# Priorities in a planned schedule, and units for two token tiles: a two-layer hybrid decoder on one core

## The chip, the cores and the metric

The kernel runs on one core of a Trainium2 chip. A core has TensorE (PE: matrix products into PSUM), VectorE (DVE), ScalarE (ACT), GpSimd (POOL), and SyncE (SP), whose queue issues nearly all the transfers here. PEld in a profile is TensorE loading the stationary operand of a matmul. The metric is the device time of one execution in microseconds; less is better.

## The reference, cut to what matters

Two layers work on 256 tokens of width 1024, in float32. Each layer does the following:

```
h = rmsnorm(x) * norm_mix
aq, ak, av, iq, ik, iw, hq, hf, hi, hg, ga, gb = split(h @ w_in)
# attention: 8 heads of 64; rope and rmsnorm on aq and ak
score = sum over 4 index heads of iw * relu(iq . ik), causal
keep the 64 best keys of each query, softmax over them, times av -> y_attn
# gated linear recurrence (hgrn): 4 heads of 128, in chunks
f = sigmoid(hf) with a lower bound, k = 1 - f, q = silu(hq), v = hi
S_t = f_t * S_(t-1) + k_t v_t ;  o_t = S_t q_t
y_hgrn = rmsnorm(o) * silu(hg)
x = x + (sigmoid(ga) * (y_attn @ w_pa) + sigmoid(gb) * (y_hgrn @ w_ph)) @ w_out
h = rmsnorm(x) * norm_ffn
x = x + (silu(h @ w_gate) * (h @ w_up)) @ w_ffn_out          # inner width 2816
```

## The kernel before

The 256 tokens are two token tiles of 128 (i = 0, 1; NT = 2 in the code). Every large matrix product is made in three passes to keep float32 accuracy: each operand is split into a part hi and a remainder lo, and hi x hi, lo x hi and hi x lo are added up in PSUM. For the activations the split is made once a layer (hT, yT, mT, h2T, act, each as hi and lo). For the weights it is made on the fly: `take()` (line 523) brings the next chunk of weights, 512 rows of 512 columns in most groups, from memory into a buffer w, ScalarE copies it rounded into hi, and VectorE subtracts to get lo. There are three buffers each for w, hi and lo. `mm3` (line 543) issues the three passes of one 128-row step.

`group` (line 755) makes one of the projections out of two chunks: idx, aq, ak, hf, hq, av, vh, hg, then ga and gb twice, in this order of the weights. For both token tiles the products of one group pile up in two accumulators, PSUM banks of tag P; there are four P banks and four Q banks. An evacuation function then takes the accumulators away with ScalarE: idx to rope and then to the index scores `dot`, aq and ak to norm and rope (`raw`, `rot`, the transposes `qkp`), hf and hq through transposes (`hfp`, `hqp`) to the recurrence, ga and gb to the gates.

The index scores of a token tile go into two Q banks; VectorE forms `work` from them and picks the 64 best by eight rounds of maximum and replace. Then come the logits (`lg`), the softmax in `lm`, its transposes `ptp` into `PT`, and the attention outputs `py`, which are split into yT. The recurrence starts with `hd` and goes through levels (`hl`, `hc`, `hx`) in which TensorE and VectorE alternate, to `po`. Both halves of yT feed `pj`, its result is transposed (`mp`) for `wo`. `out_gemm` (line 1103) does wo and, at the end of a layer, fo; as its last steps, half by half, it adds to x and calls `norm_half` (line 620: multiply by the norm's weight, four transposes xT, split into hi and lo, squares). The FFN runs over 11 blocks of 256 columns: fi, silu times up in `sl`, two transposes `fp` for each token tile, the split into `act`.

Nothing of the order is written by hand. The program is recorded first: each operation, or each `with prog.one()` block on TensorE, is one unit. `path_tails` (line 282) gives each unit the length of the longest way from it to the end, with the costs of a price table; what is not a main matmul counts 1.5 times (`stretch`). `run` (line 297) then simulates the engines: whichever unit can start first is taken, and of those that can start at the same moment on an engine the one with the largest tail plus `rank`, an added number in nanoseconds. A unit starts only when all the buffers that it takes for the first time are free. The orders that come out are fixed in the program; on the chip each engine goes through its own in that order. Small temporaries have the tag s2 (six buffers), larger ones s4 (fourteen).

Before the first data is there TensorE works on `gate`, matmuls of zeros, 28 of them (WARM, line 30). They have the lowest priority of all, so the planner puts one wherever TensorE has nothing else, and they hold one Q bank until the last is done.

The splits of the weights have rank 0 before:

```
        prog.rank = 0.0
        S.activation(hi, w, AF.Copy)
        V.tensor_tensor(lo, w, hi.bitcast(F32), op=ALU.subtract)
```

Of the kernel before, what the change touches and what calls it, by code (L numbers as in the profile page):

```python
# [13 lines left out]
AF = mybir.ActivationFunctionType  # L14
ALU = mybir.AluOpType
# [4 lines left out]
NT = T // 128  # L20
# [6 lines left out]
N_IDX = 324  # L27
C_HQ, C_HF, C_HV, C_HG, C_GA, C_GB = 1860, 2372, 2884, 3396, 3908, 4932
FIRST = {(0, C_IDX): 2, (0, C_AQ): 2}
WARM = 28  # L30
LEVELS = (2, 4, 8)
TWO_PI = 2.0 * np.pi

# [444 lines left out]
def hybrid_trunk(prog, x_d, pos_d, w_in, w_pa, w_ph, w_out, n_mix, n_ffn,  # L478
# [16 lines left out]
    def bank(name, tag="Q"):  # L495
        return prog.tile(tag, [512], F32, name)
# [21 lines left out]
                                     for o in (0, DFF)]) + ([4, 512],))  # L518
        add_rows(w_fo, l, 2, 1024, 0)

    state = {"used": 0}

    def take():
        c = state["used"]
        state["used"] += 1
        a, b, kn = chunks[c]
        k, n = kn or b
        wt, ht, lt = "w" if k * n > 1024 else "s4", "hi", "lo"
        w = prog.tile(wt, [k, n], F32, f"w{c}")
        hi = prog.tile(ht, [k, n], F32R, f"hi{c}")  # L530
        lo = prog.tile(lt, [k, n], F32R, f"lo{c}")
        prog.rank = 5e5 - 1e3 * c
        if kn is None:
            SP.dma_start(w, a)
        else:
            SP.dma_start(w[:, :, 0:256], a)
            SP.dma_start(w[:, :, 256:512], b)
        prog.rank = 0.0
        S.activation(hi, w, AF.Copy)
        V.tensor_tensor(lo, w, hi.bitcast(F32), op=ALU.subtract)  # L540
        return hi, lo

    def mm3(acc, h, hk, wc, wk, wsl, start, stop):
# [57 lines left out]
    def split_to(hi_ap, lo_ap, src, scale=None):  # L601

        if scale is None:
            S.activation(hi_ap, src, AF.Copy)
            V.tensor_tensor(lo_ap, src, hi_ap.bitcast(F32), op=ALU.subtract)
        else:
            S.activation(hi_ap, src, AF.Copy, scale=scale)
            V.scalar_tensor_tensor(lo_ap, src, scale, hi_ap.bitcast(F32), op0=ALU.mult, op1=ALU.subtract)
# [144 lines left out]
    def layer(l, hT, R):  # L753
        last = l == DEPTH - 1
        def group(n, name, evac, kk=4):
            accs = [bank(f"{name}{i}_{l}", "P") for i in range(NT)]
            for c in range(8 // kk):
                wc = take()
                for i in range(NT):
                    for k in range(kk):  # L760
                        kt = c * kk + k
                        mm3(accs[i][:, :n], hT[i], kt, wc, k, slice(0, n), kt == 0, kt == 7)
            for i in range(NT):
                evac(i, accs[i][:, :n])
# [17 lines left out]

        group(N_IDX, "idx", ev_idx, FIRST.get((l, C_IDX), 4))
        bias = []
        for i in range(NT):
            W = (i + 1) * 128
            pds = [bank(f"dot{i}{p}") for p in range(2)]
            with prog.one():
                for j in range(2):
                    for p in range(2):  # L790
                        sl = slice(64 * p, 64 * p + 64)
                        PE.matmul(pds[p][:, j * W:(j + 1) * W], idxT[sl, j, i * 128:(i + 1) * 128], idxT[sl, 2, 0:W],
                                  start=True, stop=True)
            rels = []
            for p in range(2):
                rel = tmp(f"rel{i}{p}", [2, W])
                S.activation(rel, pds[p][:, 0:2 * W].rearrange("p (a b) -> p a b", a=2), AF.Relu)
                rels.append(rel)
            work = prog.tile("work", [256], F32, f"work{i}")[:, :W]
            V.scalar_tensor_tensor(work, rels[0][:, 0, :], idxw[i][:, 0:1], neg[:, 256 - W:256], op0=ALU.mult, op1=ALU.add)  # L800
            for h in range(1, 4):
                V.scalar_tensor_tensor(work, rels[h % 2][:, h // 2, :], idxw[i][:, h:h + 1], work, op0=ALU.mult, op1=ALU.add)
            for r in range(TOPK // 8):
                m8 = small(f"m8{i}")
                V.max(m8[:, 0:8], work)
                V.match_replace(out=work, in_to_replace=m8[:, 0:8], in_values=work, imm_value=REPL)
            b = prog.tile("bias", [256], F32, f"bias{i}")[:, :W]
            V.scalar_tensor_tensor(b, work, REPL, vis[:, 256 - W:256], op0=ALU.is_equal, op1=ALU.mult)
            V.tensor_scalar(b, b, -1.0, BIG, op0=ALU.add, op1=ALU.mult)
            bias.append(b)  # L810
# [28 lines left out]
        group(512, "aq", ev_qk(0, qT), FIRST.get((l, C_AQ), 4))  # L839
        load_g(f"f{l}", n_ffn[l])  # L840
        group(512, "ak", ev_qk(1, kT))


        PT = []
# [73 lines left out]
        def ev_to(dst):  # L918
            def ev(i, acc):
                S.activation(dst[:, i, :], acc, AF.Copy, scale=R[i][:, 0:1])  # L920
            return ev

        group(512, "av", ev_to(av))
        for i in range(NT):
            py = bank(f"py{i}")
            for hp0 in (0, 2):
                with prog.one():
                    for hp in range(hp0, hp0 + 2):
                        for j in range(i + 1):
                            for p in range(2):  # L930
                                h = 2 * hp + p
                                PE.matmul(py[64 * p:64 * p + 64, hp * 128:(hp + 1) * 128], av[:, j, h * 64:(h + 1) * 64],
                                          PT[i][j][:, h, :], start=j == 0, stop=j == i)
            split_to(yT[i][0][:, 0:4, :], yT[i][1][:, 0:4, :], py.rearrange("p (k t) -> p k t", k=4))


        A = big("A", [NT, 4, 128])
# [131 lines left out]
            split_to(yT[i][0][:, 4:8, :], yT[i][1][:, 4:8, :], pv, gc)  # L1069


        gates = {}

        def ev_gate(key):
# [28 lines left out]
        def out_gemm(n_chunks, lhs, gkey, hT_out, name):  # L1103

            accs = [[bank(f"{name}{i}{g}", "Q") for g in range(2)] for i in range(NT)]
            for c in range(n_chunks - 2):
                wc = take()
                for i in range(NT):
                    for k in range(2):
                        (hh, hl), hk = lhs(i, 2 * c + k)  # L1110
                        with prog.one(main=True):
                            for g in range(2):
                                gs = slice(g * 512, (g + 1) * 512)
                                PE.matmul(accs[i][g], hh[:, hk, :], wc[0][:, k, gs], start=c == 0 and k == 0, stop=False)
                                PE.matmul(accs[i][g], hh[:, hk, :], wc[1][:, k, gs], start=False, stop=False)
                            for g in range(2):
                                gs = slice(g * 512, (g + 1) * 512)
                                PE.matmul(accs[i][g], hl[:, hk, :], wc[0][:, k, gs], start=False, stop=False)
            wcs = [take(), take()]
            Rn = []  # L1120
            for i in range(NT):
                ssq = small(f"{name}ss{i}")
                for g in range(2):
                    for c in range(2):
                        for k in range(2):
                            kt = 2 * (n_chunks - 2 + c) + k
                            h, hk = lhs(i, kt)
                            mm3(accs[i][g], h, hk, wcs[c], k, slice(g * 512, (g + 1) * 512), kt == 0, c == 1 and k == 1)
                    xs = x[:, i, g * 512:(g + 1) * 512]
                    V.tensor_tensor(xs, xs, accs[i][g], op=ALU.add)  # L1130
                    if hT_out is not None:
                        norm_half(i, g, gkey, hT_out, ssq, "P")
                    else:
                        SP.dma_start(out_d[0, i * 128:(i + 1) * 128, g * 512:(g + 1) * 512], xs)
                if hT_out is not None:
                    Rn.append(norm_scale(ssq, f"{name}r{i}"))
            return Rn
# [8 lines left out]
        for j in range(11):  # L1146
            accs = [bank(f"fi{i}", "P") for i in range(NT)]
            at = big(f"act{j}", [NT, 2, 2, 128], F32R)
            for c in range(2):
                wc = take()  # L1150
                for i in range(NT):
                    for k in range(4):
                        mm3(accs[i], h2T[i], c * 4 + k, wc, k, slice(0, 512), c == 0 and k == 0, c == 1 and k == 3)
            for i in range(NT):
                pt = bank(f"fp{j}{i}", "Q")
                sl_ = tmp(f"sl{i}", [256])
                S.activation(sl_, accs[i][:, 0:256], AF.Silu, scale=R2[i][:, 0:1])
                V.scalar_tensor_tensor(sl_, accs[i][:, 256:512], R2[i][:, 0:1], sl_, op0=ALU.mult, op1=ALU.mult)
                transpose4(pt, sl_, 2)
                split_to(at[:, i, 0], at[:, i, 1], pt[:, 0:256].rearrange("p (k t) -> p k t", k=2))  # L1160
            acts.append(at)

        hT_n = None if last else pair(f"hT{l + 1}")
# [48 lines left out]
```

## Time and profile before

| | |
|---|---|
| median of 3 runs | 814.75 us (814.44 to 815.56) |
| the profiled execution | 815.19 us, its span 813.4 us |
| TensorE busy | 801.3 us (99%) |
| weight loads (PEld) busy | 657.3 us (81%) |
| VectorE busy | 537.6 us (66%) |
| ScalarE busy | 400.9 us (49%) |
| GpSimd busy | 6.5 us (1%) |
| moved by DMA | 139.66 MB, 172 GB/s in the mean |

The span runs from the first to the last instruction. Busy times are shares of it. All operations are recorded by one helper, so all have line 467 and are told apart by the names of their tiles. A matmul row's duration reaches into the next one, since they are pipelined; the distance from start to start is what it takes from the engine. Layer 0 reaches from 0 to about 410 us, layer 1 from there to the end.

### The profile page before, as it was taken

To read this page: it belongs to the slowest core of one execution; us is meant where nothing else is said; L and a number is where in the kernel's file an instruction comes from. 1 tells how busy PE (TensorE), PEld (TensorE's weight loads), DVE (VectorE), ACT (ScalarE), POOL (GpSimd) and SP (SyncE) were. 2 spreads that over 40 slices of the span, in tenths; PEclk is the share of its full clock that TensorE was granted. 3 is DMA by queue.
4 is the path that set the end of the run, shared out by engine and by line. 5 is a ranking of instruction groups with operands and counts; after the bars stand their busy time and mean duration, and the time that the engine had idled before them with its cause. 6 is when DMAs were issued, how large, how long until landed. Compare 5 with 4: busy or idle time off the path is not lost.

```text
span 813.4 us, 10251 instructions
## 1 busy us (share of the span) xinstructions
PE 801.3 (99%) x3986; PEld 657.3 (81%) x3986; DVE 537.6 (66%) x936; ACT 400.9 (49%) x506; POOL 6.5 (1%) x8
## 2 busy tenths in 40 slices
PE   8989999999999999999999999999999999999998
PEld 7767788888888888888887778888888888888886
DVE  6999856577775455554489997566868645556442
ACT  5764855344364435453356667533445544445330
POOL 3000000000000000000000000000000000000000
PEclk9998999999999999999999999999999999999999
DMA  9725555333656656536546356443354665655531
GB/s 319 248 69 176 186 188 174 104 124 129 219 176 206 195 169 203 170 144 222 168 154 219 111 201 207 155 156 105 108 202 156 206 204 168 199 177 186 169 142 52
DMA packets 86793, 139.66 MB, mean 172 GB/s; under 512 B 3269, under 2 KB 51033, under 8 KB 86745
## 3 DMA queue, kind: packets, MB, share of 16 engines
q1 hardware_dynamic: 86584, 138.94, 51.4%
q8 instruction: 31, 0.51, 0.2%
q14 instruction: 18, 0.14, 0.0%
q10 hardware_dynamic: 160, 0.07, 0.0%
HBM read 137.95 MB, written 1.05 MB: 171 GB/s over the span
## 4 chain that ended last, share of the span: by engine, by line
PE 84%; DVE 10%; issue 2%; ACT 2%; DMA 0%; POOL 0%; POOLq 0%; ACTq 0%; DVEq 0%
PE fi L467 29%; PE fo L467 15%; PE pj L467 5%; PE gb L467 5%; PE wo L467 5%; PE ga L467 4%; DVE lo L467 4%; PE av L467 3%; PE hg L467 3%; PE vh L467 3%; PE hq L467 2%; DVE work L467 2%; PE aq L467 1%; ACT hi L467 1%; PE fp L467 1%
## 5 line engine op out<-in xcount | busy, mean ns | idle before, releaser
L467 DVE TENSOR_TENSOR lo<-w,hi 128x2048 fp32r<-128x2048 f32 (+3 forms) x134 | 296.4, 2212 | 218.5 <-ACT hi L467 217.9
L467 ACT ACTIVATE hi<-w 128x2048 fp32r<-128x2048 f32 (+3 forms) x134 | 247.3, 1846 | 280.7 <-PE fi L467 95.1
L467 PE MATMUL fi<-hi,h2T_hi 128*128 128x512 f32 x352 | 140.8, 400 | 0.2
L467 PE MATMUL fi<-hi,h2T_lo 128*128 128x512 f32 x352 | 137.8, 391 | 0.0
L467 PE MATMUL fi<-lo,h2T_hi 128*128 128x512 f32 x352 | 137.1, 390 | 0.0
L467 PE MATMUL fo<-hi,act 128*128 128x512 f32 x352 | 109.9, 391 | 0.0
L467 PEld LDWEIGHTS fi<-hi,h2T_lo 128*128 128x128 f32 x352 | 66.1, 188 | 15.0 <-DVE h2T_lo L467 0.7
L467 PEld LDWEIGHTS fo<-hi,act 128*128 128x128 f32 x352 | 66.1, 188 | 13.7
L467 PEld LDWEIGHTS fi<-hi,h2T_hi 128*128 128x128 f32 x352 | 66.1, 188 | 13.3 <-DVE h2T_lo L467 0.8
L467 PEld LDWEIGHTS fi<-lo,h2T_hi 128*128 128x128 f32 x352 | 66.2, 188 | 12.6
L467 PE MATMUL fo<-lo,act 128*128 128x512 f32 x176 | 68.5, 389 | 0.0
L467 PEld LDWEIGHTS fo<-lo,act 128*128 128x128 f32 x176 | 33.1, 188 | 6.6
L467 PE MATMUL gb<-hi,hT_hi 128*128 128x512 f32 x64 | 26.7, 418 | 0.0
L467 PE MATMUL wo<-hi,mT_hi 128*128 128x512 f32 x64 | 25.9, 405 | 0.0
L467 PE MATMUL pj<-hi,yT_hi 128*128 128x512 f32 x64 | 25.8, 404 | 0.0
L467 PE MATMUL ga<-hi,hT_hi 128*128 128x512 f32 x64 | 25.7, 401 | 0.0
L467 PE MATMUL wo<-lo,mT_hi 128*128 128x512 f32 x64 | 25.1, 392 | 0.0
L467 PE MATMUL gb<-hi,hT_lo 128*128 128x512 f32 x64 | 25.1, 392 | 0.0
L467 PE MATMUL gb<-lo,hT_hi 128*128 128x512 f32 x64 | 25.0, 391 | 0.0
L467 PE MATMUL ga<-hi,hT_lo 128*128 128x512 f32 x64 | 25.0, 391 | 0.0
L467 PE MATMUL pj<-hi,yT_lo 128*128 128x512 f32 x64 | 25.0, 391 | 0.0
L467 PE MATMUL pj<-lo,yT_hi 128*128 128x512 f32 x64 | 25.0, 390 | 0.0
(340 smaller groups left out, 1302.0 us busy)
## 6 DMA issues: line engine op xcount, KB each, us to landing
w<-in_w_ffn_in_dram SPq DMA_DIRECT2D x88, 512.0 KB, 4.5
w<-in_w_in_dram SPq DMA_DIRECT2D x42, 1024.0 KB, 4.9
w<-in_w_ffn_out_dram SPq DMA_DIRECT2D x22, 1024.0 KB, 4.7
w<-in_w_out_dram SPq DMA_DIRECT2D x8, 1024.0 KB, 4.7
w<-in_w_proj_attn_dram SPq DMA_DIRECT2D x4, 1024.0 KB, 4.9
w<-in_w_proj_hgrn_dram SPq DMA_DIRECT2D x4, 1024.0 KB, 4.8
w<-in_w_in_dram SPq DMA_DIRECT2D x4, 512.0 KB, 4.6
w<-in_w_in_dram SPq DMA_DIRECT2D x4, 324.0 KB, 5.5
```

Source lines behind the costliest of these rows:

```text
L467: getattr(engines[o.eng], name)(*[real(x) for x in a], **{n: real(x) for n, x in k.items()})
```

## The change

The splits of the weights of the groups hf, hq, av, vh and hg get a rank of 2e4, in both layers: `state["ahead"]` is set behind the group ak and set back ahead of the gates. The x add and the norm work in the last steps of `out_gemm` get the same rank. The index scores of both token tiles become one unit on TensorE, which takes four Q banks; the relu, `work` and top-k code behind it is unchanged. The attention outputs of both token tiles become one unit (before: two units for each tile), their splits follow it. In the FFN silu and product of both tiles come first, then all four transposes as one unit into one bank, then one split into hi and lo for both. The matmuls on zeros go from 28 to 24.

```
-WARM = 28
+WARM = 24
+AHEAD = 2e4
...
-    state = {"used": 0}
+    state = {"used": 0, "ahead": 0.0}
...
-        prog.rank = 0.0
+        prog.rank = state["ahead"]
         S.activation(hi, w, AF.Copy)
         V.tensor_tensor(lo, w, hi.bitcast(F32), op=ALU.subtract)
+        prog.rank = 0.0
...
-        for i in range(NT):
-            W = (i + 1) * 128
-            pds = [bank(f"dot{i}{p}") for p in range(2)]
-            with prog.one():
+        dots = [[bank(f"dot{i}{p}") for p in range(2)] for i in range(NT)]
+        with prog.one():
+            for i in range(NT):
+                W = (i + 1) * 128
                 for j in range(2):
                     for p in range(2):
...
-                        PE.matmul(pds[p][:, j * W:(j + 1) * W], idxT[sl, j, i * 128:(i + 1) * 128], idxT[sl, 2, 0:W],
+                        PE.matmul(dots[i][p][:, j * W:(j + 1) * W], idxT[sl, j, i * 128:(i + 1) * 128], idxT[sl, 2, 0:W],
...
         group(512, "ak", ev_qk(1, kT))
+        state["ahead"] = AHEAD
...
+        pys = [bank(f"py{i}") for i in range(NT)]
+        with prog.one():
+            for i in range(NT):
+                for hp in range(4):
+                    for j in range(i + 1):
+                        for p in range(2):
+                            h = 2 * hp + p
+                            PE.matmul(pys[i][64 * p:64 * p + 64, hp * 128:(hp + 1) * 128], av[:, j, h * 64:(h + 1) * 64],
+                                      PT[i][j][:, h, :], start=j == 0, stop=j == i)
         for i in range(NT):
-            py = bank(f"py{i}")
-            for hp0 in (0, 2):
-                with prog.one():
-                    for hp in range(hp0, hp0 + 2):
...
+        state["ahead"] = 0.0
         gates = {}
...
+                    prog.rank = AHEAD
                     xs = x[:, i, g * 512:(g + 1) * 512]
                     V.tensor_tensor(xs, xs, accs[i][g], op=ALU.add)
                     if hT_out is not None:
                         norm_half(i, g, gkey, hT_out, ssq, "P")
                     else:
                         SP.dma_start(out_d[0, i * 128:(i + 1) * 128, g * 512:(g + 1) * 512], xs)
+                    prog.rank = 0.0
...
+            sls = [tmp(f"sl{i}", [256]) for i in range(NT)]
             for i in range(NT):
-                pt = bank(f"fp{j}{i}", "Q")
-                sl_ = tmp(f"sl{i}", [256])
-                S.activation(sl_, accs[i][:, 0:256], AF.Silu, scale=R2[i][:, 0:1])
-                V.scalar_tensor_tensor(sl_, accs[i][:, 256:512], R2[i][:, 0:1], sl_, op0=ALU.mult, op1=ALU.mult)
-                transpose4(pt, sl_, 2)
-                split_to(at[:, i, 0], at[:, i, 1], pt[:, 0:256].rearrange("p (k t) -> p k t", k=2))
+                S.activation(sls[i], accs[i][:, 0:256], AF.Silu, scale=R2[i][:, 0:1])
+                V.scalar_tensor_tensor(sls[i], accs[i][:, 256:512], R2[i][:, 0:1], sls[i], op0=ALU.mult, op1=ALU.mult)
+            pt = bank(f"fp{j}", "Q")
+            with prog.one():
+                for i in range(NT):
+                    for k in range(2):
+                        PE.transpose(pt[:, (2 * i + k) * 128:(2 * i + k + 1) * 128], sls[i][:, k * 128:(k + 1) * 128], ident)
+            split_to(at[:, :, 0], at[:, :, 1], pt.rearrange("p (i k t) -> p i k t", i=2, k=2))
             acts.append(at)
```

## Rows read from the trace of the kernel before

**Rows 1.** The page, part 1: busy us (share of the span) and instructions.

```profile
PE 801.3 (99%) x3986; PEld 657.3 (81%) x3986; DVE 537.6 (66%) x936; ACT 400.9 (49%) x506; POOL 6.5 (1%) x8
```

**Rows 2.** The chain of waits: start us, us, what, with counts.

```profile
201.29 0.87 PE mp L467 x8
...
228.49 1.21 DVE h2T_lo L467 x2
...
353.77 54.43 PE fo L467 x240
```

**Rows 3.** TensorE's timeline in layer 0: start us, us, engine, operation, [idle before <-releaser].

```profile
55.41 0.60 PE L467 MATMUL hfp<-ident,hfraw 128*128 128x128 f32 x4
58.16 0.66 PE L467 MATMUL hfp<-ident,hfraw 128*128 128x128 f32 x4 [2.14 <-ACT hfraw L467]
...
60.32 0.79 PE L467 MATMUL hq<-lo,hT_hi 128*128 128x512 f32 x1 [1.28 <-DVE lo L467]
...
61.34 0.63 PE L467 MATMUL hq<-hi,hT_hi 128*128 128x512 f32 x1
...
66.46 0.44 PE L467 MATMUL hq<-hi,hT_hi 128*128 128x512 f32 x1
```

**Rows 4.** Busy times by stages: us, PE PEld DVE ACT POOL, PEclk, DMA share, GB/s.

```profile
40.00:60.00 20.00, 16.73 (x81) 13.05 (x79) 20.00 (x73) 13.60 (x16) 0.00 (x0) 0.99 0.25 83
60.00:80.00 20.00, 19.68 (x87) 15.70 (x88) 19.00 (x65) 8.55 (x11) 0.00 (x0) 0.84 0.50 160
100.00:120.00 20.00, 20.00 (x101) 16.30 (x100) 12.04 (x16) 10.66 (x13) 0.00 (x0) 1.00 0.50 160
```

**Rows 5.** ScalarE's timeline in layer 0.

```profile
43.25 1.92 ACT L467 ACTIVATE hi<-w 128x2048 fp32r<-128x2048 f32 x1 [0.76 <-PE ak L467]
...
53.51 0.69 ACT L467 ACTIVATE hfraw<-hf,r0y 128x512 f32<-128x512 f32 x1 [0.30 <-DVE rot L467]
```

**Rows 6.** VectorE's timeline in layer 0.

```profile
57.98 2.29 DVE L467 TENSOR_TENSOR lo<-w,hi 128x2048 fp32r<-128x2048 f32 x1
...
101.20 1.23 DVE L467 TENSOR_TENSOR lm<-lm,rs 128x1024 f32<-128x1024 f32 x1
```

**Rows 7.** TensorE's timeline in layer 1, after an hfp unit.

```profile
465.12 0.48 PE L467 MATMUL hq<-hi,hT_hi 128*128 128x512 f32 x1
465.87 0.50 PE L467 MATMUL hq<-lo,hT_hi 128*128 128x512 f32 x1 [0.26 <-DVE lo L467]
```

**Rows 8.** TensorE's timeline around the index scores of token tile 0, layer 1.

```profile
431.36 0.39 PE L467 MATMUL aq<-hi,hT_lo 128*128 128x512 f32 x1
431.68 0.71 PE L467 MATMUL dot<-idxT 64*128 64x128 f32 x8
432.32 0.50 PE L467 MATMUL aq<-hi,hT_hi 128*128 128x512 f32 x1
432.66 0.39 PE L467 MATMUL aq<-lo,hT_hi 128*128 128x512 f32 x1
```

**Rows 9.** TensorE's timeline in the first FFN block of layer 0.

```profile
229.15 0.50 PE L467 MATMUL fi<-hi,h2T_lo 128*128 128x512 f32 x1
229.74 0.50 PE L467 MATMUL fi<-hi,h2T_hi 128*128 128x512 f32 x1
```

**Rows 10.** TensorE's timeline at warm matmuls and at FFN transposes.

```profile
25.85 0.39 PE L467 MATMUL gate<-zero 128*128 128x256 bf16 x2
26.00 0.48 PE L467 MATMUL ak<-hi,hT_hi 128*128 128x512 f32 x1
...
49.00 0.28 PE L467 MATMUL gate<-zero 128*128 128x256 bf16 x1
...
271.80 0.38 PE L467 MATMUL fp<-ident,sl 128*128 128x128 f32 x2
...
274.80 0.38 PE L467 MATMUL fp<-ident,sl 128*128 128x128 f32 x2
```

**Rows 11.** TensorE's timeline at the softmax transposes of tile 1, layer 0.

```profile
122.41 1.04 PE L467 MATMUL ptp<-ident,lm 128*128 128x128 f32 x8
```

More of the change, by code (lines that the diff above doesn't have):

```diff
@@ L791, in layer @@
                         sl = slice(64 * p, 64 * p + 64)
-                        PE.matmul(pds[p][:, j * W:(j + 1) * W], idxT[sl, j, i * 128:(i + 1) * 128], idxT[sl, 2, 0:W],
+                        PE.matmul(dots[i][p][:, j * W:(j + 1) * W], idxT[sl, j, i * 128:(i + 1) * 128], idxT[sl, 2, 0:W],
                                   start=True, stop=True)
+        for i in range(NT):
+            W, pds = (i + 1) * 128, dots[i]
             rels = []
@@ L923, in layer @@
         group(512, "av", ev_to(av))
-        for i in range(NT):
-            py = bank(f"py{i}")
-            for hp0 in (0, 2):
-                with prog.one():
-                    for hp in range(hp0, hp0 + 2):
[L929 to L934, printed above, removed]
+        pys = [bank(f"py{i}") for i in range(NT)]
[7 more added lines that the diff above has]
+                                      PT[i][j][:, h, :], start=j == 0, stop=j == i)
+        for i in range(NT):
+            split_to(yT[i][0][:, 0:4, :], yT[i][1][:, 0:4, :], pys[i].rearrange("p (k t) -> p k t", k=4))
         A = big("A", [NT, 4, 128])
@@ L1153, in layer @@
                         mm3(accs[i], h2T[i], c * 4 + k, wc, k, slice(0, 512), c == 0 and k == 0, c == 1 and k == 3)
+            sls = [tmp(f"sl{i}", [256]) for i in range(NT)]
             for i in range(NT):
-                pt = bank(f"fp{j}{i}", "Q")
-                sl_ = tmp(f"sl{i}", [256])
-                S.activation(sl_, accs[i][:, 0:256], AF.Silu, scale=R2[i][:, 0:1])
-                V.scalar_tensor_tensor(sl_, accs[i][:, 256:512], R2[i][:, 0:1], sl_, op0=ALU.mult, op1=ALU.mult)
-                transpose4(pt, sl_, 2)
-                split_to(at[:, i, 0], at[:, i, 1], pt[:, 0:256].rearrange("p (k t) -> p k t", k=2))
+                S.activation(sls[i], accs[i][:, 0:256], AF.Silu, scale=R2[i][:, 0:1])
+                V.scalar_tensor_tensor(sls[i], accs[i][:, 256:512], R2[i][:, 0:1], sls[i], op0=ALU.mult, op1=ALU.mult)
+            pt = bank(f"fp{j}", "Q")
+            with prog.one():
+                for i in range(NT):
+                    for k in range(2):
+                        PE.transpose(pt[:, (2 * i + k) * 128:(2 * i + k + 1) * 128], sls[i][:, k * 128:(k + 1) * 128], ident)
+            split_to(at[:, :, 0], at[:, :, 1], pt.rearrange("p (i k t) -> p i k t", i=2, k=2))
             acts.append(at)
```

## Prediction

> **What bounds the kernel now.** I read the page first, then the busy table by stages, then the chain of waits, and last TensorE's timeline where the table shows a hole. The page's line gives TensorE 801.3 us busy of 813.4 [rows 1]. That looks like a full engine, but a busy time holds slow matmuls and overlapping records too, so I read start to start instead. In a stretch where nothing else is in the way, 240 matmuls of 128x512 take 54.43 us [rows 2], that is 0.2268 us each; this is TensorE's own rate at the 2.4 GHz level. Transposes stand at 0.87 us for 8, 0.109 us each [rows 2]. What lies above these two prices is lost, and only lost time can be won back, since the change takes away no matrix product that the result needs.
>
> The largest loss is in layer 0 between 55.41 and 66.46 us [rows 3]. In these 11.05 us TensorE issues 8 transposes (hfp) and 15 matmuls of group hq, which at the prices above is 0.87 + 3.40 = 4.27 us. So 6.78 us are lost, in three steps that the reader can see: the second hfp unit waits 2.14 us idle for ScalarE's hfraw, the second hq matmul waits 1.28 us idle for VectorE's lo, and after that the granted clock is at the lower level of 1.2 GHz: 12 matmuls from 61.34 to 66.46 us take 0.427 us each instead of 0.2268. The stage from 60 to 80 us has a mean granted clock of 0.84, the one before it 0.99 [rows 4].
>
> Who is late? ScalarE finished the hi part of the third chunk counted from hf (hf0, hf1, hq0) at 43.25 + 1.92 = 45.17 us [rows 5]. VectorE began its lo part only at 57.98 us [rows 6]: 12.8 us in which it did top-k, rope and newton work, since it was busy for 20.00 of 20 us [rows 4]. So it is the order on VectorE, and not a missing operand, that starves TensorE. (The chunks are counted by the hi parts: with three hi buffers, the hi part that starts at 43.25 us, when hf begins, is the third chunk in the queue.)
>
> Layer 1 has the same place with a small loss: twice, after each hfp unit, the step between two neighbouring hq matmuls is too long and ends with VectorE's lo; one is shown, 0.75 us [rows 7], the other is a little shorter.
>
> **The change part by part.** The profiled execution took 815.19 us, 1.79 us more than its span, and lies 0.44 us above the median of the runs shown. The sum is made against 815.19 and the 0.44 us is taken off at the end.
>
> (1) Priority of 2e4 (20 us in the planner's unit) for hi and lo of the chunks of hf, hq, av, vh and hg. It adds and removes no instruction. A lo of 2048 elements takes 2.2 us; with priority it starts when its hi is there, for hq0 at about 45.2 instead of 57.98 us, for hq1 some 6 us later. The work overtaken is bounded by the three hi buffers: at most three lo, 6.6 us, run ahead of top-k and rope. hq can then follow hf at once and the 6.78 us go, the slow clock with them, because TensorE no longer pauses. I take 6.5, since the two hfp units still have to be visited somewhere. Bounds: 0 (the hole moves) to 6.8. In layer 1 the gap shown is 0.75 us, less the 0.34 us that the first step after a unit of small matmuls takes without any wait [rows 8]: 0.4 us, and for both places 0.8 us, bounds 0 to 1.0.
>
> (2) The norm work and the x add ahead, at the ends of both out projections. At the entry of layer 0's FFN one step between neighbouring fi matmuls is 0.59 us [rows 9], 0.36 too long, right when VectorE does two h2T_lo in 1.21 us after a weight lo [rows 2]. With the norm's work first, the weight lo comes later; fi of the other token tile covers it (12 matmuls, 2.7 us, against 2.2 us of one lo). Two FFN entries of 0.36 make 0.7 us gained. If that cover fails, one lo stands on the path each time: 2.2 us lost. The norm into layer 1 is the same edit; I cost it at nothing, hidden by the idx and aq matmuls, with the same 2.2 us if not.
>
> (3) Both token tiles in one unit. A visit from the main matmuls to a unit of 64-row pieces costs time besides the pieces: the step into dot is 0.32 us and the step after its return 0.34 us [rows 8], against 0.2268, so 0.2 us a visit. dot goes from two visits to one in each layer: 0.4 us. py is not in my rows; its pieces are half-array pieces as well, and by dot's rows the one visit saved in each layer is another 0.4 us. FFN transposes: from one fp visit to the next are 3.00 us [rows 10] for 12 matmuls (2.72) and 2 transposes (0.22): 0.06 us a visit. The 44 transposes of a layer stand in 18 visits (14 of two as in rows 10, 4 of four that hold both tiles already), 11 will be left: 7 x 2 x 0.06 = 0.8 us. Together 1.6 us; bounds 0 (the waits for the second tile eat it) to 2.0. On ScalarE and VectorE two splits of 256 become one of 512, which is off the path in the FFN.
>
> What these units wait for: dot of tile 0 now waits for tile 1's idxT, and behind it wait ScalarE's relu and VectorE's top-k of tile 0; VectorE, with work in its queue for every one of the 20 us from 40 on [rows 4], uses that time for rope. dot now needs all four Q banks at once; the gate bank no longer holds one, because 24 warm matmuls are over in the first microseconds, where 28 had one left at 49.00 us [rows 10]. py of tile 0 waits for the softmax of tile 1.
>
> (4) Four warm matmuls fewer: two of them delay ak by 0.15 us (25.85 to 26.00), one stands between hf matmuls [rows 10]. The ak matmul behind the two waits for a lo anyway, so I take 0.1; bounds 0 to 0.3.
>
> (5) Against all this a term for new lateness. Top-k, rope and newton of layer 0 end up to 6.6 us later while TensorE is 6.5 us earlier. The spare time: VectorE's last softmax product starts at 101.20 us and lasts 1.23 [rows 6], and the transposes that read it are only issued at 122.41 us [rows 11], 20 us later, with VectorE at 12.04 of 20 us in that stage [rows 4]. 20 less 13 leaves 7 us. I take 0.8 us lost for places where the new order fits less well, between 0 and 6 (three lo short of the cover).
>
> Sum: 6.5 + 0.8 + 0.7 + 1.6 + 0.1 - 0.8 = 8.9 us. 815.19 - 8.9 - 0.44 = 805.9, say 806 us. With each term at its better bound it is near 803, with the hole half left near 809.
>
> **The Trainium skill against this.** The first wait of the hole ends with hfraw, and hfraw itself had stood 0.30 us until a VectorE instruction on rot was over [rows 5]; rot is not its operand, so that was a buffer. The Trainium skill, Perfetto Trace Analysis, Identifying Performance Opportunities, says that a gap repeating on the engine that should be saturated can mean that there is no SBUF or PSUM room for the next tile. By that rule priorities would not close the gap; the trace bears it out for 0.30 us and contradicts it for the wait on lo, which has an operand as its releaser. By the rule alone the sum would be that of the first rival.
>
> **Rivals.** *The hole moves* (chance 0.12, 809 to 813 us). The six small temporaries (s2) are held by rope's raw, rot and ropet. If rope ends up to 6.6 us later, hfraw gets its buffer at about 60 instead of 53.5 us, and the accumulators of hf are freed later. hq needs 48 x 0.2268 = 10.9 us, so av asks for these two P banks at about 66.3 us. The margin is 6 us for the first tile and less for the second, which waits in ScalarE's order too. If it is missed by 2 to 4 us, TensorE idles so long, and the clock may fall again (12 matmuls at 0.2 us extra, 2.4 us): 3 to 6 us of the 8.9 are given back.
>
> *No change* (0.05, about 814 to 816): the overtaken work has the higher rank by more than 20 us, lo stays late. Against it: lo was overtaken for 12.8 us only, and even at the stretch of 1.5 that is 19.
>
> *Slower* (0.08, above 817): the attention part comes too late. py of both tiles frees the big buffers from which A and the hgrn chain live; while it waits, only ga and gb feed TensorE. It decides from 7 us of further delay on VectorE beyond the 13 counted; each microsecond after that is one of idle TensorE, and slower in total needs 16 and more, since 8.9 were won first. For it speaks that dot and py of tile 0 both start later than now; against it the 7 us.
>
> **How the numbers follow.** The forecast has 0.75, its own range is 803 to 809. The range that should hold 8 in 10 is 803 to 811: it leaves out the bad half of the first rival, no change and slower (about 0.18 together). A difference of 0.2%, 1.6 us, is about what a measurement of this kernel can tell from no change. Faster: 0.75 + 0.12 = 0.87; within 0.2%: 0.05; slower: 0.08.
>
> **What would show it.** Right: hq follows hf in layer 0 at one matmul each 0.23 us and the granted clock of 60 to 80 us is near 1.00; lo of hq0 starts within 3 us of its hi; fp appears as units of four, 11 in a layer; no gate after the first 9 us. Wrong: a wait on hfraw or on an accumulator between 60 and 75 us; TensorE idle between 125 and 175 us with hd, hl or hc released by VectorE; a wait of the first FFN matmuls on a weight lo; dot released by a late idxT with top-k of both tiles behind it.

## The result, and the profile after

The changed kernel takes 803.3 us (median of 4 runs, 803.1 to 805.65) against 814.88 us before (4 runs, 814.44 to 815.56): a ratio of 0.9864, 95% interval 0.9844 to 0.9883. That is 11.6 us less; the prediction said 806 us and 8.9 us less. The profiled execution took 803.1 us, its span is 801.3.

The first part of the page of the changed kernel: busy us, share of the span, instructions.

```profile
PE 793.1 (99%) x3982; PEld 655.6 (82%) x3982; DVE 535.4 (67%) x914; ACT 399.3 (50%) x486; POOL 5.9 (1%) x8
```

Held against [rows 1], TensorE is at 99% in both. The 12 us don't show as a share; they show from start to start. The timeline of TensorE in layer 0, the place of [rows 3]:

```profile
54.09 0.39 PE L468 MATMUL hf<-hi,hT_lo 128*128 128x512 f32 x1
54.32 0.39 PE L468 MATMUL hq<-hi,hT_hi 128*128 128x512 f32 x1
54.55 0.39 PE L468 MATMUL hq<-lo,hT_hi 128*128 128x512 f32 x1
...
65.58 0.39 PE L468 MATMUL hq<-hi,hT_lo 128*128 128x512 f32 x1
65.80 0.39 PE L468 MATMUL av<-hi,hT_hi 128*128 128x512 f32 x1
```

hq follows hf at 0.23 us, no row carries a wait, and hq as a whole, 48 matmuls and one visit to qkp, takes 54.32 to 65.80: 11.48 us, 0.239 each, the visit counted in. hfp is not between them any more; its eight transposes stand in one visit at 85.7 us. The stages, for [rows 4] (busy us of PE, PEld, DVE, ACT, POOL, granted clock, DMA share, GB/s):

```profile
40.00:60.00 20.00, 20.00 (x93) 16.38 (x92) 20.00 (x51) 9.98 (x11) 0.00 (x0) 1.00 0.58 190
60.00:80.00 20.00, 20.00 (x104) 16.23 (x103) 20.00 (x76) 10.01 (x9) 0.00 (x0) 1.00 0.58 181
```

The same two engines behind it, for [rows 5] and [rows 6]. ScalarE:

```profile
43.41 1.90 ACT L468 ACTIVATE hi<-w 128x2048 fp32r<-128x2048 f32 x1
...
57.59 0.68 ACT L468 ACTIVATE hfraw<-hf,r0y 128x512 f32<-128x512 f32 x1
...
63.22 0.69 ACT L468 ACTIVATE hfraw<-hf,r1y 128x512 f32<-128x512 f32 x1 [0.74 <-DVE ropet L468]
```

VectorE:

```profile
45.84 2.29 DVE L468 TENSOR_TENSOR lo<-w,hi 128x2048 fp32r<-128x2048 f32 x1
51.73 2.28 DVE L468 TENSOR_TENSOR lo<-w,hi 128x2048 fp32r<-128x2048 f32 x1
...
97.50 1.23 DVE L468 TENSOR_TENSOR lm<-lm,rs 128x1024 f32<-128x1024 f32 x1
```

The hi part of hq's first chunk ends at 43.41 + 1.90 = 45.31, its lo begins 0.5 us later; before it was 12.8 us. VectorE is as full as before (20.00 of 20 us in the stage from 40 us on): it does the same work in another order. hfraw is later than before (57.59 against 53.51 us), and the second one has waited for ropet, which is the buffer wait of the prediction's first rival. TensorE does not feel it. And the work that was overtaken is not late here: the last softmax product starts at 97.50 us, before at 101.20 (with the rank of the splits alone it is late, see e1).

TensorE at the new units, for [rows 8] and [rows 10]: index scores and FFN transposes in layer 0, and the attention outputs.

```profile
29.72 1.58 PE L468 MATMUL dot<-idxT 64*128 64x128 f32 x16
31.23 0.50 PE L468 MATMUL aq<-hi,hT_hi 128*128 128x512 f32 x1
...
102.81 2.84 PE L468 MATMUL py<-PT,av 128*64 128x128 f32 x48
...
263.42 0.60 PE L468 MATMUL fp<-ident,sl 128*128 128x128 f32 x4
263.77 0.48 PE L468 MATMUL fi<-hi,h2T_hi 128*128 128x512 f32 x1
```

The fp units of four come 11 in a layer, and no gate is left after 8.2 us. The chain of waits at the first FFN, for [rows 9], is one piece from 219.99 to 263.58 us; the 0.59 us step at 229 us is gone.

```profile
219.99 43.59 PE fi L468 x192
264.02 10.93 PE fi L468 x48
275.39 10.95 PE fi L468 x48
```

To see where the time came from, the starts of the groups on TensorE are set side by side, read from the first row of each group in the timelines (us). The runs e1 and so on are the experiments below. The first microseconds differ from execution to execution: before, e5 and e6 issue the same units up to the first matmul of idx, but it starts at 8.3, 10.2 and 9.6 us, after waits of 0.17, 0.86 and 0.88 us on a transfer. So a distance from the first hf says more than a start by itself.

| first matmul of | before | after | e1 | e3 | e6 | e7 | e11 | e12 | e9 |
|---|---|---|---|---|---|---|---|---|---|
| hf, layer 0 | 43.0 | 43.0 | 43.8 | 43.8 | 44.2 | 44.0 | 42.1 | 42.0 | 41.4 |
| hq, layer 0 | 58.6 | 54.3 | 55.1 | 61.0 | 59.8 | 61.0 | 57.5 | 53.4 | 52.3 |
| av, layer 0 | 76.3 | 65.8 | 66.8 | 75.6 | 77.2 | 76.0 | 72.8 | 65.0 | 64.1 |
| wo, layer 0 | 201.9 | 194.1 | 196.3 | 200.7 | 202.8 | 201.1 | 198.8 | 194.0 | 198.1 |
| fi, layer 0 | 225.8 | 217.9 | 220.0 | 224.6 | 226.6 | 225.0 | 222.7 | 217.8 | 222.8 |
| fo, layer 0 | 351.9 | 342.9 | 346.2 | 349.6 | 352.2 | 351.1 | 348.9 | 342.8 | 348.1 |
| wo, layer 1 | 599.2 | 587.8 | 592.1 | 595.3 | 597.7 | 596.6 | 594.2 | 588.8 | 598.3 |
| fo, layer 1 | 749.2 | 736.6 | 742.1 | 744.2 | 747.1 | 746.6 | 744.2 | 737.7 | 748.0 |

After against before: 7.8 us are won up to wo of layer 0, 1.1 more in layer 0's FFN (from fi to fo 125.0 us instead of 126.1), 2.4 from there to wo of layer 1, 1.2 from there to fo of layer 1; behind it 0.5 are given back.

### The profile page after: what moved, and what is told of

Its sections match the earlier page's. It is cut to its first block, busy times and chain, and to the rows that moved or that the text cites. A ratio compares the mean times of both kernels' runs of the same rounds, so it can differ in the third digit from the quotient of the medians.

```text
span 801.3 us, 10205 instructions
## 1 busy us (share of the span) xinstructions
PE 793.1 (99%) x3982; PEld 655.6 (82%) x3982; DVE 535.4 (67%) x914; ACT 399.3 (50%) x486; POOL 5.9 (1%) x8
## 4 chain that ended last, share of the span: by engine, by line
PE 90%; DVE 7%; ACT 1%; issue 1%; DMA 0%; POOL 0%
PE fi L468 30%; PE fo L468 15%; PE gb L468 6%; PE wo L468 6%; PE pj L468 5%; PE ga L468 4%; PE vh L468 3%; PE hg L468 3%; PE av L468 3%; DVE lo L468 2%; PE aq L468 2%; PE hf L468 1%; PE hq L468 1%; PE ak L468 1%; PE fp L468 1%
```

## The experiments

Twelve kernels. In each paragraph "before" is the kernel before in runs on the same chip, 814.63 to 815.04 us; the interval is that of the ratio to it, 95%.

**e1_splits_only**: the kernel before with the rank on the splits; `state["ahead"]` is set and set back as in the change.

```
...
-        prog.rank = 0.0
+        prog.rank = state["ahead"]
         S.activation(hi, w, AF.Copy)
         V.tensor_tensor(lo, w, hi.bitcast(F32), op=ALU.subtract)
+        prog.rank = 0.0
...
```

> The kernel before with the priority of the weight splits alone (2e4 for hf, hq, av, vh, hg). Theory A (the order on VectorE starves TensorE in layer 0): the stretch from 55 to 66 us runs at 0.23 us a matmul, 6.5 to 7 us gained in layer 0 and about 1 in layer 1, so 806.5 to 808 us. Rival B (a free Q bank, from fewer warm matmuls and from the merged units, is what lets hq follow hf): the hole stays, 814 to 815 us.

807.42 us, 0.9911 (0.9897 to 0.9924): 7.2 us of the 11.6. hq follows hf at 55.1 us; hfraw comes at 63.51 and 69.12 us, later still than in the changed kernel, and av starts at 66.8 without a wait. Rival B is out: there are 28 matmuls on zeros and separate units here, and the hole is gone all the same. The softmax is late, by 11.8 us against before (VectorE's timeline of e1):

```profile
113.01 1.23 DVE L468 TENSOR_TENSOR lm<-lm,rs 128x1024 f32<-128x1024 f32 x1
```

TensorE does not feel that either: the transposes of tile 1 follow from 112.04 to 120.25 us, none with a wait.

**e2_lo_only**: the rank on VectorE's part alone.

```
...
         prog.rank = 0.0
         S.activation(hi, w, AF.Copy)
+        prog.rank = state["ahead"]
         V.tensor_tensor(lo, w, hi.bitcast(F32), op=ALU.subtract)
+        prog.rank = 0.0
...
```

> As the run before, but the priority is on VectorE's lo alone; ScalarE's hi keeps rank 0. Theory A: the lo was late and not the hi, so within 1 us of the run before, 806.5 to 808 us. Rival C (ScalarE's order, which puts hi ahead of hfraw, is half of the cause, as the 2.14 us wait on hfraw suggests): 2 to 4 us are left of the hole, 809 to 811 us.

807.77 us, 0.9915 (0.9902 to 0.9929), the same as e1. It was VectorE's order that was wrong; ScalarE's hi needs no priority.

**e3_all_but_splits**: the changed kernel with the rank of the splits back at 0.

```
...
-        state["ahead"] = AHEAD
+        state["ahead"] = 0.0
```

> The changed kernel with the rank of the weight splits set to 0; norm priority, merged units and 24 warm matmuls stay. Theory A: the hole of layer 0 comes back, 7 to 8 us above the changed kernel, 810 to 812 us, the rest of the change being worth 3 to 5 us. Rival B: within 2 us of the changed kernel, 803 to 805 us.

810.23 us, 0.994 (0.9928 to 0.9952). The hole is back, with the same kinds of waits (TensorE's timeline, layer 0):

```profile
52.24 0.50 PE L468 MATMUL hf<-lo,hT_hi 128*128 128x512 f32 x1 [1.57 <-DVE lo L468]
...
57.57 0.60 PE L468 MATMUL hfp<-ident,hfraw 128*128 128x128 f32 x4
...
60.31 1.04 PE L468 MATMUL hfp<-ident,hfraw 128*128 128x128 f32 x4 [2.14 <-ACT hfraw L468]
```

**e4_splits_5us**: e1 with 5e3 instead of 2e4.

```
+AHEAD = 5e3
...
```

> As the first run, with a rank of 5e3 in place of 2e4. Theory A with the size of the rank as the step that decides: lo of hq was overtaken for 12.8 us, so a lead of 5 us leaves part of the hole, 809 to 813 us. If any positive rank breaks the tie (rival D), it is within 0.5 us of the first run.

807.92 us, 0.9916 (0.9903 to 0.993): the same as e1. I had thought that a lead smaller than the 12.8 us by which lo was overtaken would leave it late. That was the wrong measure. The lo of hq's first chunk still starts 4.3 us later than in the changed kernel, but it ends 2.4 us before the first matmul that reads it (VectorE's and TensorE's timelines of e4):

```profile
50.13 2.27 DVE L468 TENSOR_TENSOR lo<-w,hi 128x2048 fp32r<-128x2048 f32 x1
...
54.82 0.39 PE L468 MATMUL hq<-lo,hT_hi 128*128 128x512 f32 x1
```

What counts is not how long lo has been possible, but when TensorE asks for it.

**e5_fp_only**: the kernel before with the FFN transposes of both tiles in one unit.

```
...
-                pt = bank(f"fp{j}{i}", "Q")
...
+            pt = bank(f"fp{j}", "Q")
+            with prog.one():
+                for i in range(NT):
+                    for k in range(2):
+                        PE.transpose(pt[:, (2 * i + k) * 128:(2 * i + k + 1) * 128], sls[i][:, k * 128:(k + 1) * 128], ident)
...
```

> The kernel before with the FFN transposes of both token tiles in one unit, alone. By the term of the sum (0.06 us a visit, 7 visits fewer in a layer): 0.8 us gained, 813.5 to 814.3 us, about 0.4 us in each FFN. Rival (the second tile's silu is waited for): no gain or a loss, 814.7 to 817 us.

814.39 us, 0.9994 (0.9985 to 1.0002). Not to be told from no change in the time. In the trace the FFN of layer 0, from the first fi to the first fo, is 0.5 us shorter, that of layer 1 0.6. The trace is shorter by another 1.2 us between the first hf and the first av, which the edit does not explain: VectorE's splits stand there as before, but of the hq matmuls 6 follow each other at 0.43 us and not 13.

**e6_norms_only**: the kernel before with the rank on the x add and the norm work.

```
...
+                    prog.rank = AHEAD
                     xs = x[:, i, g * 512:(g + 1) * 512]
...
+                    prog.rank = 0.0
```

> The kernel before with the priority of the x add and the norm work alone. By the term of the sum: 0.36 us at each FFN entry and nothing at the entry of layer 1, 813.7 to 814.3 us. If the rank also helps the entry of layer 1, 1 us or more is gained between the last fo matmul of layer 0 and pj of layer 1, 812.5 to 813.5 us. Rival (the weight lo that is pushed back stands on the path): 815 to 819 us.

812.12 us, 0.9967 (0.9955 to 0.9979): 2.8 us (1.7 to 3.7 by the interval), four times the 0.7 of my sum. The FFNs are each some 0.5 us shorter for their entry, more than the 0.36 of one step. From layer 0's first fo to layer 1's first hf, which I had costed at nothing, 0.5 us are won. The largest part lies behind that, in layer 1's attention: from the first hf of layer 1 (446.1 us here, 446.4 before) to its first av (471.6, 473.1) it is 1.2 us. The two steps at lo around hfp are gone [rows 7]; the transposes now stand in one visit, with nothing behind them late (TensorE's timeline, layer 1):

```profile
463.47 1.03 PE L468 MATMUL hfp<-ident,hfraw 128*128 128x128 f32 x8
464.26 0.48 PE L468 MATMUL hq<-hi,hT_hi 128*128 128x512 f32 x1
464.58 0.40 PE L468 MATMUL hq<-lo,hT_hi 128*128 128x512 f32 x1
```

The lo of this place has rank 0 here, and starts at 462.00 instead of 463.53 us. How the norms' rank brings that about is not shown: the lo at 436.13 us is still no earlier than before (435.97), the next one is (446.39 against 447.85). As far as it goes, part of what the norms bring is what the splits' rank brings too; no run has these two without the rest.

**e7_units_only** and **e11_dot_only**: the kernel before with 24 gate matmuls and one unit for dot; e7 has one for py as well.

```
-WARM = 28
+WARM = 24
...
+        dots = [[bank(f"dot{i}{p}") for p in range(2)] for i in range(NT)]
+        with prog.one():
+            for i in range(NT):
...
+        pys = [bank(f"py{i}") for i in range(NT)]
+        with prog.one():
+            for i in range(NT):
...
```

> The kernel before with the index scores and the attention outputs in one unit each and 24 warm matmuls; no priority, FFN as before. By the terms of the sum: 0.9 us, 813.5 to 814.2 us, with the hole of layer 0 still there. Rival (tile 0's top-k, later by the wait for tile 1, adds to the work in front of lo): the hole grows by 1 to 3 us, 815 to 818 us.

> The kernel before with the index scores of both tiles in one unit and 24 warm matmuls; attention outputs as before. The run with both units gained 2.1 us where the sum had 0.9. If the visits alone make it (0.2 us each), this run has about half of the gain of visits, 0.5 us, 814.0 to 814.6 us. If the two dot units in one let the order behind them fall better in layer 1, 1 us or more is gained ahead of the group hq of layer 1, 812.5 to 813.8 us.

e7 took 812.8 us, 0.9976 (0.9961 to 0.9991); e11, with less of the change, 810.46 us, 0.9958 (0.9944 to 0.9972). Both gained more than I had expected. The merged py seems to cost 2 us, but that is not shown: the intervals overlap, and e7's eleven runs lie between 811.06 and 816.5 us. Nor do the traces show it. Of the 2.6 us between their spans 1.8 are there at the first hf, 1.2 of them at the first matmul of idx, 9.15 against 7.92 us. From the first vh (90.4 and 87.7 us), which is ahead of py, to the first wo the two take 110.7 and 111.2 us. What differs between hf and vh is the order on VectorE, 40 us ahead of py. e7 has the lo parts at 50.13 and 58.99 us and the hole of e3; e11 has them at 55.25 and 63.29 and a smaller hole, in another place (TensorE's timeline of e11):

```profile
54.01 0.60 PE L467 MATMUL hfp<-ident,hfraw 128*128 128x128 f32 x4
...
56.75 1.12 PE L467 MATMUL hfp<-ident,hfraw 128*128 128x128 f32 x4 [2.14 <-ACT hfraw L467]
...
65.64 0.50 PE L467 MATMUL hq<-lo,hT_hi 128*128 128x512 f32 x1 [0.93 <-DVE lo L467]
```

An edit to one unit can alter the order of all that stands ahead of it, since the planner's tails are added up from the end. With rank 0 on the splits the merged units do that here: from the first hf to the first hq it is 15.5 us in before, e5 and e6, 15.4 in e11, but with the hole in another place, and 17.0 and 17.2 in e7 and e3. In the six kernels with the rank (after, e1, e2, e4, e10, e12) it is 10.9 to 11.4, whatever else they change. The edits of e5 and e6, far behind this place, left it as it was.

**e12_after_py_split**: the changed kernel with py in two units a tile, as before.

```
...
-        pys = [bank(f"py{i}") for i in range(NT)]
...
+            py = bank(f"py{i}")
+            for hp0 in (0, 2):
+                with prog.one():
...
```

> The changed kernel with the attention outputs in two units a tile, as before; all else of the change stays. Alone, the index scores in one unit gained 4.2 us (814.63 to 810.46), the index scores and the attention outputs together only about 2 us (0.9976), so the merged attention outputs cost some 2 us there. Theory: they cost as much in the changed kernel, since one unit of 48 matmuls waits for the softmax of both tiles whatever else is done: 801 to 802 us. Rival G: with the splits ahead, TensorE has main matmuls of av and vh in front of the attention outputs and the wait is covered: 803 to 804, no difference from the changed kernel. In both cases the outputs show as 16 and 32 matmuls of py, or in halves of these, with main matmuls between them.

803.9 us, 0.9868 (0.9851 to 0.9884), the same as the changed kernel. So my theory fell, and rival G's result stands: with the splits ahead the merged py costs nothing, and gains nothing that the times show.

**e8_s2_8** and **e9_after_s2_8**: eight small temporaries instead of six, in the kernel before and in the changed one.

```
-SLOTS = {... "s2": 6, ...
+SLOTS = {... "s2": 8, ...
```

> The kernel before with eight small temporaries (s2) instead of six. Theory A: the wait for lo stays, since its order on VectorE is by the tails; at most the wait on hfraw shortens, 813 to 815 us. Rival E (the hole is a want of buffers, the rule of repeating gaps): 808 to 811 us.

> The changed kernel with eight small temporaries instead of six. In the kernel before, eight cost 13 us, because lo stayed away from VectorE for 24 us (43.47 to 67.36 us) while attention work came first. Theory A: with the priority on the splits that cannot happen, so the 13 us are gone, within 2 us of the changed kernel, 801 to 806 us. Rival F (more temporaries hurt for another reason, late products in front of wo and late transposes): 808 us and more.

e8 took 827.77 us, 1.0152 (1.0139 to 1.0165), which neither theory had. The rule of the Trainium skill, Perfetto Trace Analysis, Identifying Performance Opportunities (a repeating gap can mean that there is no room for the next tile), does not help here: with more room the hole did not close, it moved one chunk on. hq now follows hf at 54.83 us, with its first lo in time, and the lo of its second chunk is the late one. VectorE's timeline of e8, two lo parts that follow each other:

```profile
43.47 2.28 DVE L467 TENSOR_TENSOR lo<-w,hi 128x2048 fp32r<-128x2048 f32 x1
...
67.36 2.27 DVE L467 TENSOR_TENSOR lo<-w,hi 128x2048 fp32r<-128x2048 f32 x1
```

24 us lie between them. VectorE spent them on top-k (40 instructions that write work), rope (13 that write rot or ropet) and newton; in the 11 us between the two lo parts at 46.91 and 57.98 us of the kernel before it was 12 and 7. TensorE starved meanwhile; its longest wait there is 3.97 us, for n11y, a piece of newton on VectorE:

```profile
60.00:80.00 20.00, 14.57 (x79) 11.29 (x79) 19.00 (x60) 10.14 (x16) 0.00 (x0) 0.83 0.26 77
```

That the two buffers let this work start early is the reading that fits; that more of it stood ahead of the split is measured. By that reading the buffers had been a limit on how far VectorE strayed from what TensorE needs. But this hole is the smaller part of e8's 13 us, as the next run lets one see.

e9 took 814.72 us, 0.9998 (0.9989 to 1.0007): all of the gain is lost again. I had expected 801 to 806, since with the rank the splits are on time whatever the buffers. They are: lo starts at 43.74, 49.47 and 55.09 us, av at 64.1, 12 us ahead of before and 1.7 ahead of the changed kernel. But wo starts 4.0 us behind the changed kernel in layer 0 and 10.5 behind in layer 1, and in front of wo the same thing happens the other way round. TensorE's timeline of e9:

```profile
192.61 1.51 PE L468 MATMUL mp<-ident,ma 128*128 128x128 f32 x12
196.86 0.66 PE L468 MATMUL mp<-ident,ma 128*128 128x128 f32 x4 [2.75 <-DVE ma L468]
198.06 0.80 PE L468 MATMUL wo<-hi,mT_hi 128*128 128x512 f32 x1 [0.54 <-DVE mT_lo L468]
198.66 0.63 PE L468 MATMUL wo<-lo,mT_hi 128*128 128x512 f32 x1
199.08 0.63 PE L468 MATMUL wo<-hi,mT_hi 128*128 128x512 f32 x1
```

And VectorE's of e9, then of the changed kernel:

```profile
193.92 2.28 DVE L468 TENSOR_TENSOR lo<-w,hi 128x2048 fp32r<-128x2048 f32 x1
196.12 0.68 DVE L468 TENSOR_TENSOR ma<-ma,mb 128x512 f32<-128x512 f32 x1
```

```profile
192.75 0.68 DVE L468 TENSOR_TENSOR ma<-ma,mb 128x512 f32<-128x512 f32 x1
193.35 2.29 DVE L468 TENSOR_TENSOR lo<-w,hi 128x2048 fp32r<-128x2048 f32 x1
```

In e9 a weight split that nobody waits for yet stands ahead of the last ma, for which all of TensorE waits; in the changed kernel it is the other way round. At the prices of 0.2268 and 0.109 us a piece this place costs e9 5.2 us, the slow clock behind the pauses included (the steps from 192.61 on, against 16 transposes and the wo matmuls up to 201.19 us), and the same place in layer 1 costs 4.8: 10.0 of the 11.4 us that e9 is behind the changed kernel.

e8 has the same order in front of wo, in both layers; the kernel before has no such wait. TensorE's and VectorE's timelines of e8:

```profile
207.06 1.11 PE L467 MATMUL mp<-ident,ma 128*128 128x128 f32 x4 [2.75 <-DVE ma L467]
...
204.13 2.28 DVE L467 TENSOR_TENSOR lo<-w,hi 128x2048 fp32r<-128x2048 f32 x1
...
206.33 0.68 DVE L467 TENSOR_TENSOR ma<-ma,mb 128x512 f32<-128x512 f32 x1
```

At the same prices it costs e8 6.2 and 5.4 us, 11.6 of its 13. So my expectation for e9 laid the 13 us to the wrong place, and the splits' rank, which does not reach this one, could not win them back. Why two more buffers turn the order round here is not shown.

**e10_after_all_ahead**: the changed kernel with the rank on every split, those of idx, aq, ak, the gates and the FFN too.

```
-    state = {"used": 0, "ahead": 0.0}
+    state = {"used": 0, "ahead": AHEAD}
...
-        state["ahead"] = 0.0
```

> The changed kernel with the rank of 2e4 on every weight split, those of idx, aq, ak, the gates, the projections and the FFN too. What is left to win are the waits on a weight lo near 8, 15, 21 and 27 us and in the fo groups, 0.45 us each: 801 to 803.5 us. Rival: splits that run ahead push back the silu products and the norms, 804 to 807 us.

803.72 us, 0.9867 (0.9853 to 0.988): no difference from the changed kernel, and neither the gain that I expected nor the rival's loss.

## Why the prediction was right

The forecast held in sign, in its range, and in the mechanism of its largest term; the sum was 2.7 us short. That the range held is partly luck. At their better bounds the prediction's own terms add up to 6.8 + 1.0 + 0.7 + 2.0 + 0.3 = 10.8 us, which gives 804.0 and not "near 803"; the measured 803.3 lies beyond that. Term (2), which measured alone is four times its size, is the likely reason, and the range took the time in because its end was set a microsecond lower than the terms give. Step by step:

**What bounds the kernel: right.** TensorE's lost time, read from start to start, was what could be won, and the largest loss was the hole of [rows 3], made by the order on VectorE. e2 shows the last part by itself: one number added to one VectorE instruction brings 6.9 us.

**(1) The splits, 6.5 + 0.8 us: right.** Alone they bring 7.2 us (e1). In e1's trace 6.3 are won from the first hf to wo of layer 0 (against 6.5), and 1.3 from fo of layer 0 to wo of layer 1 (against 0.8). The slow clock went with the waits, as argued: the stage from 60 to 80 us has a granted clock of 1.00 in the changed kernel, and hq runs through.

**(2) The norms, 0.7 us: right in kind, too small.** Alone 2.8 us (e6). The two FFN entries gave about 0.5 us each instead of 0.36. The norm into layer 1, which I cost "at nothing, hidden by the idx and aq matmuls", is the term that was mis-sized: 0.5 us up to the first hf and 1.2 from there to the first av, where in the kernel before a lo was late [rows 7]. By which steps in VectorE's order the norms' rank moves that lo is open.

**(3) The units, 1.6 us: mixed.** The fp part was about right: 0.8 predicted, 0.5 and 0.6 in the traces of the two FFNs, too little for the measured time to show. dot and py at 0.4 each can't be confirmed. dot with 24 gates brought 4.2 us alone, 2.5 of them between the first hq and the first av of layer 0, by way of the hole; with py as well it brought 2.1 (0.7 to 3.2 by the interval); py by itself, in the changed kernel, nothing that the times show (e12). The price of a visit is borne out for fp alone; what the merged dot did to the order behind it was several times as large as its visits, and the sum had no term for it.

**(4) Four gate matmuls fewer, 0.1 us.** Not to be seen: hf of layer 0 starts at 43.0 us in both. No run had this edit alone.

**(5) New lateness, 0.8 us: it came on VectorE and cost TensorE nothing.** With the rank of the splits alone the last softmax product of layer 0 starts 11.8 us later (e1), nearly twice the 6.6 that I had bounded by the three hi buffers, so that bound was wrong; it stayed within the 20 us of spare time. In the changed kernel it starts 3.7 us earlier than before. The merged units bring that: without the rank e3 and e7 have it at 95.77 and 96.16 us. py of both tiles was done by 105.7 us, where tile 1's softmax transposes were only issued at 122.41 before [rows 11].

Of the four, 7.2 + 2.8 + 2.1 + 0.5 = 12.6 us alone; the change as a whole brings 11.6. The difference is within the intervals; an overlap at the lo waits of both layers fits it but is not shown. Of the 4.1 us by which the change is ahead of the splits alone (e1), the traces put 2.3 in the two FFNs.

**The rivals.** *The hole moves*: its mechanism came, hfraw late and released by ropet, but not its price, because TensorE takes hfp only at 85.7 us; I had asked when the P banks come free, and av found them free even in e1, with hfraw at 63.51 and 69.12 us. *No change* and *slower*: neither came. The Trainium skill's rule on room (Perfetto Trace Analysis, Identifying Performance Opportunities), weighed in the prediction, did not describe this gap: more room moved it by a chunk (e8), and an order on VectorE closed it (e2).

What stays open: how the norms' rank moves the lo of layer 1, why eight temporaries turn the order in front of wo, and whether dot's merging is worth anything in the changed kernel. No version beat the changed kernel.

## What to carry to other kernels

When the bounding engine waits for an operand that was ready to be made long ago, look at the order on the engine that makes it: a priority on that one instruction can be worth more than all edits that save instructions. In a kernel whose order a planner makes, judge an edit in the version in which the known holes are closed: before that, an edit can shift the hole, and its time alone (here 4.2 us for dot, 2.1 for dot and py) says little of its own cost. And more buffers are not harmless: with two more, the planner put a split that nobody waited for yet ahead of a product for which all of TensorE waited.

## What the runs showed of the hardware

A wait can cost more than its length. In e9, after pauses of 2.75 and 0.54 us, the next wo matmuls stand 0.42 to 0.43 us apart, at the lower of the two levels, from 198.66 us on; they are back at 0.23 from 201.19 us (granted clock 0.50 in the stage from 198 to 201 us, 0.98 from 201 to 204). The waits of 0.2 to 0.6 us in the first 22 us of the changed kernel leave the granted clock at 1.00, and behind the 0.93 us of e11 the matmuls stand 0.23 us apart again after one step. For the hole of [rows 3] the slow matmuls were 12 x 0.2 = 2.4 of the 6.78 us. That share is not fixed: with the same two waits there, e6's trace has 11 steps of 0.43 us and e5's 6, where the kernel before has 13.
